# RMSNorm and matmul on one core: casts in groups of eight and four tiles, roots for eight tiles, squares four pairs ahead, no SyncE drains

## The chip, the core and the metric

The kernel runs on one core of a Trainium2 chip. A core has five engines with programs of their own. TensorE multiplies matrices, VectorE (DVE in a profile) and ScalarE (ACT) work on tiles element by element, GpSimd (POOL) is a programmable engine, and SyncE (SP) here only issues transfers. Sixteen DMA engines move data between the chip's memory (HBM) and the core's SBUF. Matmuls write to PSUM, a second small memory. The metric is the device time of one execution in microseconds, the median of several runs. The profile's span is a little shorter than that time, since it runs from the first to the last recorded event.

## The reference

Each of 16 x 1024 rows of 512 numbers is divided by its root mean square, multiplied by gamma, and multiplied by a 512 x 768 matrix:

```python
batch, seq, dim, out_dim = 16, 1024, 512, 768

def reference(x, gamma, weight, eps):
    rms = np.sqrt(np.mean(x ** 2, axis=-1, keepdims=True) + eps)
    x_norm = x / rms * gamma
    return np.matmul(x_norm, weight).astype(np.float32)
```

The input x is 33.6 MB of float32 and the output 50.3 MB.

## The kernel before

The rows are cut into 128 tiles of 128 rows, and the tiles into 64 pairs; a step j of the main loop multiplies pair j, tiles 2j and 2j+1. The division by the root mean square commutes with the matmul, so it is applied when a result leaves PSUM. Gamma is multiplied into the weights once.

A tile goes this way. SyncE loads it as float32, in groups of 16 tiles (`XG`), some groups in one transfer and some in two of eight tiles. GpSimd casts it to bf16. TensorE transposes it, two bf16 at a time seen as one float32 word, and VectorE copies the result from PSUM to SBUF. TensorE multiplies: four blocks of 128 features, each in a part of 512 and one of 256 columns. ScalarE (even tiles) or VectorE (odd tiles) scales the result on its way out of PSUM, and SyncE stores eight tiles at a time. Meanwhile ScalarE squares and sums each tile, takes the root of the means, and VectorE takes the reciprocal.

From the second group on, the last four tiles of each 16 (a "quad") take another way: GpSimd casts them in one instruction and VectorE transposes them in SBUF in 16 moves, three per step.

```python
xin = ctx.enter_context(tc.tile_pool(name="xin", bufs=2))
xbp = ctx.enter_context(tc.tile_pool(name="xb", bufs=4))
stats = ctx.enter_context(tc.tile_pool(name="stats", bufs=4))
tpsum = ctx.enter_context(tc.tile_pool(name="tpsum", bufs=2, space=bass.MemoryType.PSUM))
opsum = ctx.enter_context(tc.tile_pool(name="opsum", bufs=3, space=bass.MemoryType.PSUM))
outp = ctx.enter_context(tc.tile_pool(name="out", bufs=3))
# ... (cut)
def cast(i, engine, n=1):
    if i // 2 not in xb_tiles:
        xb_tiles[i // 2] = xbp.tile([P, 2, D], BF16, name="xb")
    engine.tensor_copy(out=xb_tiles[i // 2][:, i % 2:i % 2 + n, :], in_=held(x_tiles, XG, i, n))

def square(i, ssq):
    jk = junk.tile([P, D], BF16, name="jk")
    nc.scalar.activation(out=jk, in_=held(x_tiles, XG, i)[:, 0, :], func=AF.Square, accum_out=ssq)

def root(i, n, ssq):
    rms = stats.tile([P, 4], F32, name="rms")
    nc.scalar.activation(out=rms[:, :n], in_=ssq[:, :n], func=AF.Sqrt, scale=1.0 / D, bias=eps_sb)
    rstd = stats.tile([P, 4], F32, name="rstd")
    nc.vector.reciprocal(out=rstd[:, :n], in_=rms[:, :n])
    # ... (cut)
# ... (cut)
    load_until(2)
    load_weights(0)
    load_weights(1)
    load_until(2 * XG)
    for _ in range(20):
        nc.sync.drain()
# ... (cut: tiles 0 and 1)
    for j in range(1, NP):
        load_until((2 * j + AHEAD + XG - 1) // XG * XG)
        if j + 3 < NP and quad_of(j + 3) is None:
            cast(2 * j + 6, nc.gpsimd, 2)
        if (2 * j + 2) % XG == 0 and 2 * j + 2 < NT:
            cast_quad((2 * j + 2 + XG - 4) // 4)
        elif 2 * j >= XG:
            move_quad(3)
        if j < 4:
            norms(2 * j + 2, 2)
        if 3 <= j < NP - 2:
            norms_by_four(j + 2)      # squares of pair j+2; a root after every second pair
        if j < 3:
            feed = feeder([j + 1], mid if j == 1 else one, alone=j == 1)
        elif j == 3:
            feed = feeder([4, 5], both)
        elif j + 2 < NP and quad_of(j + 2) is None:
            feed = feeder([j + 2], two)       # transposes of pair j+2 between the matmuls
        else:
            feed = None
        for i, engine in ((2 * j, nc.scalar), (2 * j + 1, nc.vector)):
            a = accumulator()
            matmuls(i, a, range(K), feed)
            finish_tile(i, a, engine)
```

Each engine works through its own program in order. So a ScalarE instruction that waits for data also holds up the evictions behind it, and a TensorE transpose that waits for a cast also holds up the matmuls behind it.

Of the kernel before, what the change touches and what calls it, by code (L numbers as in the profile page):

```python
# [12 lines left out]
F32 = mybir.dt.float32  # L13
BF16 = mybir.dt.bfloat16
# [4 lines left out]
def kernel(  # L19
# [8 lines left out]
    nc = tc.nc  # L28
    P = 128

    x = x.flatten_outer_dims()
    out = out.flatten_outer_dims()
    N, D = x.shape
    _, O = out.shape
    K = D // P
    NT = N // P
    NP = NT // 2
    XG, OG = 16, 8
# [23 lines left out]

    singles = ctx.enter_context(tc.tile_pool(name="singles", bufs=1))
    xin = ctx.enter_context(tc.tile_pool(name="xin", bufs=2))
    xbp = ctx.enter_context(tc.tile_pool(name="xb", bufs=4))
    junk = ctx.enter_context(tc.tile_pool(name="junk", bufs=2))
    stats = ctx.enter_context(tc.tile_pool(name="stats", bufs=4))
    xt_pool = ctx.enter_context(tc.tile_pool(name="xt", bufs=4))
# [6 lines left out]
    x_tiles, xb_tiles, tp_tiles, rstd_of, xT_tiles, o_tiles, norm_sums = {}, {}, {}, {}, {}, {}, {}  # L75

    def held(tiles, group, i, n=1):
        return tiles[i // group][:, i % group:i % group + n, :]
# [8 lines left out]
    def load_until(i):  # L87
        while starts and starts[0] < i:
            load(starts.pop(0))

    def cast(i, engine, n=1):
        if i // 2 not in xb_tiles:
            xb_tiles[i // 2] = xbp.tile([P, 2, D], BF16, name="xb")
        engine.tensor_copy(out=xb_tiles[i // 2][:, i % 2:i % 2 + n, :], in_=held(x_tiles, XG, i, n))  # L94

    def square(i, ssq):
        jk = junk.tile([P, D], BF16, name="jk")
        nc.scalar.activation(out=jk, in_=held(x_tiles, XG, i)[:, 0, :], func=AF.Square, accum_out=ssq)  # L98

    def root(i, n, ssq):  # L100
        rms = stats.tile([P, 4], F32, name="rms")
        nc.scalar.activation(out=rms[:, :n], in_=ssq[:, :n], func=AF.Sqrt, scale=1.0 / D, bias=eps_sb)  # L102
        rstd = stats.tile([P, 4], F32, name="rstd")
        nc.vector.reciprocal(out=rstd[:, :n], in_=rms[:, :n])  # L104
        for t in range(n):
            rstd_of[i + t] = rstd[:, t:t + 1]

    def norms(i, n):
        ssq = stats.tile([P, 4], F32, name="ssq")
        for t in range(n):  # L110
            square(i + t, ssq[:, t:t + 1])
        root(i, n, ssq)


    def norms_by_four(j):
        if j % 2:
            norm_sums[j] = stats.tile([P, 4], F32, name="ssq")
        ssq = norm_sums[j - (j + 1) % 2]
        for t in range(2):
            square(2 * j + t, ssq[:, 2 * (1 - j % 2) + t:2 * (1 - j % 2) + t + 1])  # L120
        if j % 2 == 0:
            root(2 * j - 2, 4, ssq)
        elif j == NP - 1:
            root(2 * j, 2, ssq)

    def transpose_word(j, t, h):
        if j not in tp_tiles:
            tp_tiles[j] = tpsum.tile([P, 2, 2, P], F32, name="tp")  # L130
        words = xb_tiles[j].rearrange("p a d -> p (a d)").bitcast(F32)
        lo = t * (D // 2) + h * P
        nc.tensor.transpose(out=tp_tiles[j][:, t, h, :], in_=words[:, lo:lo + P], identity=ident_f)  # L133

    def evac(j, t=0, n=2):
# [7 lines left out]
    def transpose_tile(i):  # L143
        for h in range(2):
            transpose_word(i // 2, i % 2, h)
        evac(i // 2, i % 2, 1)
# [6 lines left out]
    def quad_of(j):  # L153
        return j // 2 if (2 * j) % XG >= XG - 4 and 2 * j >= XG else None
# [14 lines left out]
    def move_quad(n):  # L169
        for _ in range(min(n, len(quad_moves))):  # L170
            dst, src = quad_moves.pop(0)
            nc.vector.transpose(out=dst, in_=src)  # L172

    def scale(engine, dst, src, r):
        if engine is nc.scalar:
            nc.scalar.mul(out=dst, in_=src, mul=r)  # L176
        else:
            nc.vector.tensor_single_scalar(out=dst, in_=src, scalar=r, op=mybir.AluOpType.mult)  # L178

    def accumulator():  # L180
        return opsum.tile([P, 2, WIDE], F32, name="ops").rearrange("p a b -> p (a b)")
# [16 lines left out]
    def matmuls(i, acc, ks, feed=None):  # L198
        for k in ks:
            matmul(i, k, acc, 0, WIDE)  # L200
            if feed:
                feed()
            matmul(i, k, acc, WIDE, O)

    def finish_tile(i, acc, engine):
        scale(engine, out_tile(i), acc[:, :O], rstd_of[i])
        store(i)
# [16 lines left out]
    with tc.manual_schedule():  # L224
        g_row = singles.tile([2, P, 2], F32)
        nc.scalar.dma_start(out=g_row, in_=gamma.rearrange("(h w c) -> h w c", w=P, c=2))
        nc.scalar.preload_act_table(AF.Sqrt)  # L227
        wv = weight.rearrange("(h w c) o -> w h (c o)", w=P, c=2)
        w_f32 = singles.tile([P, K, O], F32)

        def load_weights(h):
            nc.sync.dma_start(out=w_f32[:, 2 * h:2 * h + 2, :].rearrange("p c o -> p (c o)"), in_=wv[:, h, :])  # L232

        load_until(2)
        load_weights(0)
        load_weights(1)
        load_until(2 * XG)

        for _ in range(20):
            nc.sync.drain()  # L240


        warm = singles.tile([P, WIDE], BF16)
        nc.vector.memset(warm, 0.0)
        eps_sb = singles.tile([P, 1], F32)
        nc.vector.memset(eps_sb, float(eps))  # L246
        ident_f = singles.tile([P, P], F32)
        make_identity(nc, ident_f)
        spare = accumulator()

        def warm_up(n):
            for _ in range(n):
                nc.tensor.matmul(out=spare[:, :WIDE], lhsT=warm[:, :P], rhs=warm, start=True, stop=True)  # L253

        w_bf = singles.tile([P, K, O], BF16)

        def weights(k, engine, lo=0, hi=O):
            scale(engine, w_bf[:, k, lo:hi], w_f32[:, k, lo:hi], g_sb[:, k % 2, k // 2:k // 2 + 1])


        warm_up(6)
        gp = tpsum.tile([P, 2, 2], F32, name="tp")
        for c in range(2):
            nc.tensor.transpose(out=gp[:, c, :], in_=g_row[:, :, c], identity=ident_f[:2, :2])  # L264
        g_sb = singles.tile([P, 2, 2], F32)
        nc.vector.tensor_copy(out=g_sb, in_=gp)  # L266
        cast(0, nc.gpsimd)
        cast(1, nc.gpsimd)
        cast(2, nc.gpsimd, 2)
        norms(0, 2)  # L270
        warm_up(4)
        transpose_tile(0)
        transpose_tile(1)
        warm_up(2)
        weights(0, nc.vector, 0, WIDE)
        weights(0, nc.vector, WIDE, O)
        weights(1, nc.scalar)
        acc = [accumulator() for _ in range(2)]
        for i in range(2):
            matmuls(i, acc[i], [0, 1])  # L280
        weights(2, nc.vector)
        weights(3, nc.scalar)
        norms(2, 2)
        cast(4, nc.gpsimd)
        cast(5, nc.gpsimd)
        matmuls(0, acc[0], [2, 3])
        finish_tile(0, acc[0], nc.scalar)
        matmuls(1, acc[1], [2, 3], feeder([1], [2, 2], alone=True))
        finish_tile(1, acc[1], nc.vector)
        cast(6, nc.gpsimd, 2)  # L290

        mid, one, two, both = ([0, 0, 1, 1, 0, 1, 1, 0], [1, 1, 0, 1, 1, 0, 0, 0], [1, 0, 1, 0, 1, 0, 1, 0],
                               [1, 1, 1, 1, 1, 1, 1, 1])
        for j in range(1, NP):
            load_until((2 * j + AHEAD + XG - 1) // XG * XG)
            if j + 3 < NP and quad_of(j + 3) is None:
                cast(2 * j + 6, nc.gpsimd, 2)
            if (2 * j + 2) % XG == 0 and 2 * j + 2 < NT:
                cast_quad((2 * j + 2 + XG - 4) // 4)
            elif 2 * j >= XG:  # L300
                move_quad(3)
            if j < 4:
                norms(2 * j + 2, 2)
            if 3 <= j < NP - 2:
                norms_by_four(j + 2)
            if j < 3:
                feed = feeder([j + 1], mid if j == 1 else one, alone=j == 1)
            elif j == 3:
                feed = feeder([4, 5], both)
            elif j + 2 < NP and quad_of(j + 2) is None:  # L310
                feed = feeder([j + 2], two)
# [6 lines that stand above are left out]
# [35 lines left out]
```

## Time and profile before

| | before |
|---|---|
| time, median of 3 runs | 210.53 us (210.35 to 210.74) |
| span of the profiled run | 208.4 us |
| granted TensorE clock, mean | 0.985 |
| moved by DMA | 85.68 MB, mean 411 GB/s |
| GpSimd casts of pairs and single tiles | 52, 51.3 us |
| squares on ScalarE | 128, 79.1 us |
| roots on ScalarE, reciprocals on VectorE | 35 and 35, 10.5 and 6.1 us |
| SyncE drains | 20, from 4.6 to 5.7 us |

How to read the lines. In a timeline the columns are the start in us, the length in us, the engine, the line of the kernel, the operation, the output and inputs by their names with shapes, how many instructions are merged, and in brackets how long the engine had been idle and what released it. PE is TensorE and PEld its loading of stationary operands. In the kernel before, L94 is the cast, L98 the square, L102 the root, L104 the reciprocal, L133 the transpose, L140 its copy out of PSUM, L172 the moves of a quad, L176 and L178 the scaling on ScalarE and VectorE, L191 the stores, L194 the matmuls and L83 the loads of x. A group's line gives count, busy time, mean of one in ns, and the idle time before with its releasers. The chain of waits follows back from the last instruction to what released it.

### The profile page before, as it was taken

The page shows a single profiled execution, that of the slowest core. Times are in us where ns is not written, and L with a number is a line of the kernel's source. Part 1 is how long each engine was busy: PE and PEld are TensorE (multiplying, and loading weights), DVE is VectorE, ACT ScalarE, POOL GpSimd, SP SyncE. Part 2 cuts the span into 40 slices and gives each one's busy share as a digit, 9 for nine tenths or more (in the row PEclk, how much of TensorE's full clock was granted, in tenths as well). Part 3 has the DMA queues.
Part 4 walks back from the last instruction along what each step waited for, and adds up shares of the span by engine and source line. Part 5 has one row for each costly group of instructions (what it writes and reads, how often), then busy time and mean ns, then how long its engine had stood idle before and what let it go on. Part 6 is the DMA issues. An engine that isn't in the chain of part 4 may idle for free.

```text
span 208.4 us, 3474 instructions
## 1 busy us (share of the span) xinstructions
PE 193.8 (93%) x1238; PEld 129.3 (62%) x1238; DVE 150.8 (72%) x270; ACT 149.8 (72%) x358; POOL 64.7 (31%) x65
## 2 busy tenths in 40 slices
PE   7699999998999999999999999999999999999800
PEld 3367767764766667666766667666776666766400
DVE  0465657997399957998499957998499957998300
ACT  4698787778678787778778887778778885887300
POOL 3247554002920383055210563016510265000000
PEclk9999999999999999999999999999999999999985
DMA  6999999999999999999999999999999999998992
GB/s 251 421 435 443 343 391 436 463 429 399 417 445 434 410 439 417 418 448 424 432 423 424 437 421 439 418 421 435 440 431 410 442 428 434 437 410 354 419 417 104
DMA packets 5493, 85.68 MB, mean 411 GB/s; under 512 B 610, under 2 KB 612, under 8 KB 1380
## 3 DMA queue, kind: packets, MB, share of 16 engines
q1 hardware_dynamic: 5472, 85.46, 97.0%
q8 instruction: 9, 0.15, 0.3%
q14 instruction: 8, 0.07, 0.1%
q10 hardware_dynamic: 4, 0.00, 0.0%
HBM read 35.13 MB, written 50.33 MB: 410 GB/s over the span
## 4 chain that ended last, share of the span: by engine, by line
PE 78%; DMA 14%; POOL 1%; DVE 1%; SPq 1%; issue 1%; POOLq 0%
PE ops L194 69%; DMA xt<-in_x_dram 14%; PE tp L133 9%; POOL xb L94 1%; DVE ot L178 1%; SPq L232 0%; SPq L83 0%; SPq L191 0%; POOLq L94 0%; DVE xT L140 0%
## 5 line engine op out<-in xcount | busy, mean ns | idle before, releaser
L194 PE MATMUL ops<-w_bf,xT 128*128 128x512 bf16 (+1 forms) x800 | 147.6, 326 | 1.0 <-DVE w_bf L178 0.8
L194 PEld LDWEIGHTS <-xT 128*128 128x128 bf16 x800 | 78.3, 98 | 46.9 <-issue 1.1
L176 ACT ACTIVATE ot<-ops,rstd 128x768 f32<-128x768 f32 x64 | 57.7, 902 | 41.6 <-PE ops L194 39.3
L94 POOL CAST xb<-xt 128x1024 bf16<-128x1024 f32 (+1 forms) x52 | 51.3, 1010 | 98.9 <-DMA xt<-in_x_dram 50.1
L98 ACT ACTIVATE jk<-xt 128x512 bf16<-128x512 f32 x128 | 79.1, 622 | 1.9 <-DMA xt<-in_x_dram 1.7
L178 DVE TENSOR_SCALAR ot<-ops,rstd 128x768 f32<-128x768 f32 x64 | 64.6, 1010 | 9.5 <-PE ops L194 9.1
L133 PE MATMUL tp<-ident_f,xb 128*128 128x128 f32 x200 | 53.9, 273 | 1.4 <-POOL xb L94 1.4
L140 DVE COPY xT<-tp 128x1024 bf16<-128x1024 bf16 (+1 forms) x53 | 34.7, 656 | 25.2 <-PE tp L133 24.5
L172 DVE STREAM_TRANSPOSE xTq<-xq 32x256 f32<-32x256 f32 x112 | 48.7, 435 | 1.9
L194 PE MATMUL ops<-w_bf,xTq 128*128 128x512 bf16 x224 | 42.8, 326 | 0.0
L133 PEld LDWEIGHTS tp<-ident_f,xb 128*128 128x128 f32 x200 | 28.0, 141 | 5.1 <-POOL xb L94 2.6
L194 PEld LDWEIGHTS <-xTq 128*128 128x128 bf16 x224 | 22.0, 98 | 12.4
L98 ACT ACTIVATION_READ_ACCUMULATOR jk<-xt 128x1 f32 x128 | 24.6, 192 | 0.0
L158 POOL CAST xq<-xt 128x2048 bf16<-128x2048 f32 x7 | 13.3, 1896 | 11.4 <-DMA xt<-in_x_dram 9.6
L102 ACT ACTIVATE rms<-ssq,eps_sb 128x4 f32<-128x4 f32 (+1 forms) x35 | 10.5, 299 | 1.1
L104 DVE RECIPROCAL rstd<-rms 128x4 f32<-128x4 f32 (+1 forms) x35 | 6.1, 175 | 6.3 <-ACT rms L102 5.5
L253 PE MATMUL ops<-warm 128*128 128x512 bf16 x12 | 4.4, 505 | 1.2 <-DVE eps_sb L246 1.2
L176 ACT ACTIVATE w_bf<-w_f,g_sb 128x768 bf16<-128x768 f32 x2 | 1.9, 937 | 1.3 <-DMA w_f<-in_weight_dram 1.3
L253 PEld LDWEIGHTS <-warm 128*128 128x128 bf16 x12 | 1.2, 118 | 2.5 <-DVE eps_sb L246 1.2
L266 DVE COPY g_sb<-tp 128x4 f32<-128x4 f32 x1 | 0.2, 164 | 3.2 <-PE tp L264 3.2
L227 ACT ACT_TABLE_LOAD x1 | 1.3, 1283 | 1.3 <-PEq L334 1.3
L178 DVE TENSOR_SCALAR w_bf<-w_f,g_sb 128x512 bf16<-128x512 f32 (+2 forms) x3 | 1.4, 483 | 0.8 <-DMA w_f<-in_weight_dram 0.8
(10 smaller groups left out, 1.9 us busy)
## 6 DMA issues: line engine op xcount, KB each, us to landing
out_dram<-ot SPq DMA_DIRECT2D x13, 3072.0 KB, 18.4
xt<-in_x_dram SPq DMA_DIRECT2D x11, 2048.0 KB, 18.9
xt<-in_x_dram SPq DMA_DIRECT2D x2, 4096.0 KB, 21.4
out_dram<-ot SPq DMA_DIRECT2D x5, 1536.0 KB, 10.9
w_f<-in_weight_dram SPq DMA_DIRECT2D x2, 768.0 KB, 5.5
out_dram<-ot SPq DMA_DIRECT2D x2, 768.0 KB, 17.0
xt<-in_x_dram SPq DMA_DIRECT2D x2, 512.0 KB, 5.1
xt<-in_x_dram SPq DMA_DIRECT2D x1, 1024.0 KB, 9.1
```

What stands on the lines that cost most here:

```text
L94: engine.tensor_copy(out=xb_tiles[i // 2][:, i % 2:i % 2 + n, :], in_=held(x_tiles, XG, i, n))
L98: nc.scalar.activation(out=jk, in_=held(x_tiles, XG, i)[:, 0, :], func=AF.Square, accum_out=ssq)
L102: nc.scalar.activation(out=rms[:, :n], in_=ssq[:, :n], func=AF.Sqrt, scale=1.0 / D, bias=eps_sb)
L104: nc.vector.reciprocal(out=rstd[:, :n], in_=rms[:, :n])
L133: nc.tensor.transpose(out=tp_tiles[j][:, t, h, :], in_=words[:, lo:lo + P], identity=ident_f)
L140: nc.vector.tensor_copy(out=dst[:, t:t + n, :], in_=src[:, t:t + n, :])
L158: nc.gpsimd.tensor_copy(out=quads[q], in_=held(x_tiles, XG, 4 * q, 4))
L172: nc.vector.transpose(out=dst, in_=src)
L176: nc.scalar.mul(out=dst, in_=src, mul=r)
L178: nc.vector.tensor_single_scalar(out=dst, in_=src, scalar=r, op=mybir.AluOpType.mult)
L194: nc.tensor.matmul(out=acc[:, lo:hi], lhsT=xT_tiles[i // 2][:, i % 2, k // 2, :, k % 2], rhs=w_bf[:, k, lo:hi], start=(k == 0), stop=(k == ...
L253: nc.tensor.matmul(out=spare[:, :WIDE], lhsT=warm[:, :P], rhs=warm, start=True, stop=True)
```

## The change

The change makes three engines' programs shorter. GpSimd casts eight tiles with one instruction, and the four that are left of a group before its quad with another; the bf16 buffers become two of eight tiles instead of four of two. ScalarE takes one root for eight tiles (ten at the end) in place of four, and VectorE one reciprocal. For that, the squares run four pairs ahead of the matmuls instead of two, so that the last pair of a group of roots is squared before the first is needed. The 20 drains on SyncE go.

```diff
-    xbp = ctx.enter_context(tc.tile_pool(name="xb", bufs=4))
+    xbp = ctx.enter_context(tc.tile_pool(name="xb", bufs=2))
@@ cast: tiles of the bf16 buffer
-        if i // 2 not in xb_tiles:
-            xb_tiles[i // 2] = xbp.tile([P, 2, D], BF16, name="xb")
-        engine.tensor_copy(out=xb_tiles[i // 2][:, i % 2:i % 2 + n, :], in_=held(x_tiles, XG, i, n))
+        if i // 8 not in xb_tiles:
+            xb_tiles[i // 8] = xbp.tile([P, 8, D], BF16, name="xb")
+        engine.tensor_copy(out=xb_tiles[i // 8][:, i % 8:i % 8 + n, :], in_=held(x_tiles, XG, i, n))
@@ squares and roots (ssq, rms and rstd become [P, 10])
-    def norms_by_four(j):
-        ...
+    NORM_GROUPS = [(5, 2), (7, 4)] + [(f, 4) for f in range(11, NP - 5, 4)] + [(NP - 5, 5)]
+    norm_first = {f + n: (f, s) for f, s in NORM_GROUPS for n in range(s)}
+    norm_turns = {3: [5], 4: [6], 5: [7, 8], 6: [9, 10], **{j: [j + 4] for j in range(7, NP - 6)}, NP - 6: [NP - 2, NP - 1]}
+
+    def norms_of_group(j):
+        first, size = norm_first[j]
+        if j == first:
+            norm_sums[first] = stats.tile([P, 10], F32, name="ssq")
+        ssq = norm_sums[first]
         for t in range(2):
-            square(2 * j + t, ...)
+            square(2 * j + t, ssq[:, 2 * (j - first) + t:2 * (j - first) + t + 1])
+        if j == first + size - 1:
+            root(2 * first, 2 * size, ssq)
@@ after the first loads
-        for _ in range(20):
-            nc.sync.drain()
@@ before the main loop
-        cast(4, nc.gpsimd)
-        cast(5, nc.gpsimd)
+        cast(4, nc.gpsimd, 2)
@@ in the main loop
-            if j + 3 < NP and quad_of(j + 3) is None:
-                cast(2 * j + 6, nc.gpsimd, 2)
+            if j == 1:
+                cast(8, nc.gpsimd, 8)
+            elif j % 8 == 4 and j + 4 < NP:
+                cast(2 * j + 8, nc.gpsimd, 8)
+            elif j % 8 == 6 and j + 2 < NP:
+                cast(2 * j + 12, nc.gpsimd, 4)
...
-            if 3 <= j < NP - 2:
-                norms_by_four(j + 2)
+            for pair in norm_turns.get(j, []):
+                norms_of_group(pair)
```

Cut in this diff: the tile shapes of `root` and `norms`, the body of `norms_by_four`, and the new index of `transpose_word` into the larger bf16 buffer.

More of the change, by code (lines that the diff above doesn't have):

```diff
@@ L100, in root @@
     def root(i, n, ssq):
-        rms = stats.tile([P, 4], F32, name="rms")
+        rms = stats.tile([P, 10], F32, name="rms")
         nc.scalar.activation(out=rms[:, :n], in_=ssq[:, :n], func=AF.Sqrt, scale=1.0 / D, bias=eps_sb)
-        rstd = stats.tile([P, 4], F32, name="rstd")
+        rstd = stats.tile([P, 10], F32, name="rstd")
         nc.vector.reciprocal(out=rstd[:, :n], in_=rms[:, :n])
@@ L108, in norms @@
     def norms(i, n):
-        ssq = stats.tile([P, 4], F32, name="ssq")
+        ssq = stats.tile([P, 10], F32, name="ssq")
         for t in range(n):
@@ L112, in norms @@
         root(i, n, ssq)
-    def norms_by_four(j):
-        if j % 2:
-            norm_sums[j] = stats.tile([P, 4], F32, name="ssq")
-        ssq = norm_sums[j - (j + 1) % 2]
-        for t in range(2):
[L120 to L124, printed above, removed]
+    NORM_GROUPS = [(5, 2), (7, 4)] + [(f, 4) for f in range(11, NP - 5, 4)] + [(NP - 5, 5)]
[6 more added lines that the diff above has]
+        ssq = norm_sums[first]
+        for t in range(2):
+            square(2 * j + t, ssq[:, 2 * (j - first) + t:2 * (j - first) + t + 1])
+        if j == first + size - 1:
+            root(2 * first, 2 * size, ssq)
     def transpose_word(j, t, h):
@@ L130, in transpose_word @@
             tp_tiles[j] = tpsum.tile([P, 2, 2, P], F32, name="tp")
-        words = xb_tiles[j].rearrange("p a d -> p (a d)").bitcast(F32)
-        lo = t * (D // 2) + h * P
+        words = xb_tiles[j // 4].rearrange("p a d -> p (a d)").bitcast(F32)
+        lo = (j % 4 * 2 + t) * (D // 2) + h * P
         nc.tensor.transpose(out=tp_tiles[j][:, t, h, :], in_=words[:, lo:lo + P], identity=ident_f)
```

## The prediction

> **What bounds the kernel now.** I read the page first, then the chain of waits, then the stretches where the chain leaves TensorE. Page, parts 1 and 2:
>
> ```profile
> PE 193.8 (93%) x1238; PEld 129.3 (62%) x1238; DVE 150.8 (72%) x270; ACT 149.8 (72%) x358; POOL 64.7 (31%) x65
> DMA  6999999999999999999999999999999999998992
> GB/s 251 421 435 443 343 391 436 463 429 399 417 445 434 410 439 417 418 448 424 432 423 424 437 421 439 418 421 435 440 431 410 442 428 434 437 410 354 419 417 104
> ```
>
> Two resources are nearly full at once, TensorE and the DMA queue; ScalarE, VectorE and GpSimd, where the change removes instructions, are at 72, 72 and 31%. The chain of waits is TensorE from 10.32 us to 197.46 us with one break:
>
> ```profile
> 27.56 1.02 DVE ot L178
> ...
> 28.63 0.33 SPq L191
> ...
> 29.07 21.39 DMA xt<-in_x_dram
> ...
> 50.60 1.05 POOL xb L94
> ...
> 51.70 0.33 PE tp L133
> ```
>
> The reader is to see a 16-tile load (tiles 32 to 47) issued at 29.07, landing at 50.46, a cast of two of its tiles, and TensorE's transposes of pair 16 starting as that cast ends. TensorE waited 0.7 us there (list of waits). Away from it, a step of two tiles takes 3.04 us with four transposes and 2.60 us without, which is the time of its own matmuls.
>
> The other place is the start, in the timeline of GpSimd (start, us, then what; in brackets the wait before) and of TensorE:
>
> ```profile
> 16.70 4.00 POOL L94 CAST xb<-xt 128x1024 bf16<-128x1024 f32 x4 [2.83 <-DMA xt<-in_x_dram]
> 17.79 0.14 PEld L133 LDWEIGHTS tp<-ident_f,xb 128*128 128x128 f32 x1 [0.16 <-POOL xb L94]
> ```
>
> The load of tiles 8 to 15 lands at about 16.65; the first two-tile cast ends at 17.74, and TensorE takes it 0.05 us later. TensorE and GpSimd are exactly just-in-time here too.
>
> The end, by windows (start:end, length, busy us of each engine, clock, DMA share, GB/s):
>
> ```profile
> 188.00:190.00 2.00, 2.00 (x14) 1.18 (x12) 1.91 (x5) 1.64 (x4) 0.00 (x0) 1.00 0.63 270
> 200.00:202.00 2.00, 0.00 (x0) 0.00 (x0) 0.00 (x0) 0.00 (x0) 0.00 (x0) 1.00 1.08 455
> 188.57 5.10 SPq L191 DMA_DIRECT2D out_dram<-ot  x2
> ```
>
> The queue runs dry at 188 until the store of tiles 112 to 119 is issued at 188.57 (the third line, SyncE's timeline), and is then full until past 204: 3072 + 1536 + 1536 KB, 6.3 MB, at some 430 GB/s are 14.6 us. So the end is fixed by when tile 119 is finished. If TensorE slips, the end slips with it; if TensorE came earlier, the queue would still be busy with the older stores until 188 and nearly nothing would be won.
>
> **What the Trainium skill says.** "Perfetto Trace Analysis", Optimizing Scalar/DVE Operations: grouping into larger operations helps if the engine is saturated, and if it isn't but causes bubbles elsewhere, breaking instructions up lets work finish sooner. GpSimd at 31% is the second case, and this change groups. "DMA: Bandwidth & Descriptors", Queues, rings and completion order: on each DMA engine descriptors are consumed in ring order. The trace agrees: the load of 29.07 took 21.39 us for 4 MB, 10 us at the rate seen, because older work stood before it. "SBUF — State Buffer", SBUF: two separate sides: a GpSimd and a VectorE instruction can block each other for a whole instruction on a shared port. No sign of it here: every two-tile cast takes 1041 to 1045 ns.
>
> **The change part by part.** Groups by form give the price of a cast:
>
> ```profile
> L94 POOL CAST xb<-xt 128x1024 bf16<-128x1024 f32 x48 | 49.0, 1042 | 94.7 <-DMA xt<-in_x_dram 45.9 <-PE tp L133 26.0 <-PE ops L194 22.8
> L158 POOL CAST xq<-xt 128x2048 bf16<-128x2048 f32 x7 | 13.3, 1896 | 11.4 <-DMA xt<-in_x_dram 9.6 <-DVE xTq L172 1.8
> L94 POOL CAST xb<-xt 128x512 bf16<-128x512 f32 x4 | 2.3, 615 | 4.1 <-DMA xt<-in_x_dram 4.1
> ```
>
> From 1024 to 2048 elements 0.854 us more, so 4096 elements take 1.896 + 2 x 0.854 = 3.60 us (estimate). Casts of this line go from 52 to 20 (2 of one tile, 3 of two, 8 of eight, 7 of four): 1.2 + 3.1 + 28.8 + 13.3 = 46.5 us instead of 51.3. GpSimd waits for data anyway, so the 4.8 us are worth nothing; the granularity counts. A consumer of the first pair now waits 3.60 us after the landing instead of 1.04: +2.56 us, wherever the first pair was just in time.
>
> (a) Start, tiles 4 and 5: one cast of 1.04 instead of two of 0.61, the first transpose 0.4 us later; swallowed by (b).
> (b) Start, pair 4: the cast of tiles 8 to 15 ends at 16.70 + 3.60 = 20.30 instead of 17.74. TensorE stands for 2.56 us. Everything after is 2.56 us later (estimate).
> (c) Pair 16. The load's landing does not move although its issue does. By 29.07 SyncE had issued 14.7 MB (32 tiles of x 8.39, weights 1.57, stores of tiles 0 to 11 4.72). Windows up to 29 us give 10.9 MB moved (334, 442, 422, 377, 320 GB/s over 10, 7, 4, 4, 4 us). So 3.8 MB, 9 us of work, stand before the load; issuing it 2.56 us later changes nothing, and it still lands at 50.46. The cast of tiles 32 to 39 then ends at 50.60 + 3.60 = 54.20, transposes at 54.30 instead of 51.70: +2.6 us. TensorE by itself would be there at 51.70 - 0.7 + 2.56 = 53.56, so it waits 0.7 us again. The two delays overlap; they do not add.
> (d) Squares four pairs ahead. ScalarE's timeline before:
>
> ```profile
> 44.09 0.90 ACT L176 ACTIVATE ot<-ops,rstd 128x768 f32<-128x768 f32 x1 [0.91 <-PE ops L194]
> 44.89 0.62 ACT L98 ACTIVATE jk<-xt 128x512 bf16<-128x512 f32 x1
> ...
> 46.91 0.90 ACT L176 ACTIVATE ot<-ops,rstd 128x768 f32<-128x768 f32 x1 [0.36 <-PE ops L194]
> ...
> 50.54 0.63 ACT L98 ACTIVATE jk<-xt 128x512 bf16<-128x512 f32 x1
> ...
> 51.91 0.30 ACT L102 ACTIVATE rms<-ssq,eps_sb 128x4 f32<-128x4 f32 x1
> ```
>
> The evictions are those of tiles 22 and 24 (so step 12 began at 46.91 - 0.05 - 1.30 = 45.5 on TensorE), the squares at 44.89 those of step 12, those at 50.54 the squares of pair 16 in step 14. With the change pair 16 comes in step 12, at 44.89 + 2.56 = 47.5, and ScalarE stands until 50.54, with the eviction of tile 24 behind. Two squares take 1.3 us (50.54 to the root at 51.91, less its gap), the eviction 0.90: done at 52.75. Three accumulators rotate, so tile 27 needs the one of tile 24. TensorE would start tile 27 at 45.5 + 2.56 + 3 x 1.30 = 51.96; it waits 0.8 us, ends tile 27 at 54.1 and meets the transposes of pair 16 at 54.3. That is the same instant as in (c): again an overlap.
> (e) Later groups. Slack grows, because loads are bound by the queue and TensorE is now 2.6 us later. Eight steps take 6 x 3.04 + 2 x 2.60 = 23.44 us; step 14 begins at 51.4, so step 20 at 69.65. Pair 24: data at 71.30 (GpSimd's timeline, like the next), step 20 now at 69.65 + 2.6 = 72.3, so ScalarE does not wait; the cast ends at 74.9 and the transposes come at 77.8. Tightest after that is the last group: data at 165.19, step 52 at 69.65 + 4 x 23.44 + 2.6 = 166.0.
> (f) Roots: 35 to 20, 15 x 0.30 us on ScalarE and 15 x 0.175 us on VectorE. 4.5 and 2.6 us of busy time; each has idle time in most steps. VectorE is full only while it moves quads (5.8 of 6 us in 34 to 46); there two of three reciprocals go, 0.35 us per group, and TensorE was not waiting for it.
> (g) The 20 drains run from 4.6 to 5.7 us, after the last early load is issued at 4.5 and 7 us before the first store at 12.77: nothing.
>
> Sum: 2.6 us on the path. Span 208.4 to 211.0; the time is 2.1 us above the span before, so **213.1 us**, a ratio of 1.012.
>
> **The rivals.** First: the delays add, (b) 2.6 and (c) or (d) 2.6 more less the 0.7, 4.5 us, 215.0 us. This needs the landing of the 16-tile load to move with its issue. Its issue does hang on tile 11 (chain), but 3.8 MB of older work speak against it; I give it 7%. Second: the pool is faster with one long cast, or its landing is earlier than I read, so that the wait is nearer 1.9 us, (b) alone less the 0.7 us gap: 212.4. This happens if the last packets of the load land a little earlier, which the queue allows, since by windows it moved only 354 and 395 GB/s in 46 to 48 and 48 to 50 us. Third: the shorter programs relieve something that bounds (ScalarE, VectorE), and the kernel gains. Against it: TensorE has 0.7 us of waiting after 10.3, and the queue holds old stores until 188, so at most some 0.5 us could come: 210.0. Fourth: deeper squares free the input buffer earlier, so loads are issued earlier (SyncE waited 7.7 us in all for ScalarE before loads, at most 1.6 at once). But data already arrives early and the queue is full: hidden.
>
> **Range and chances.** The 2.6 us rest on one extrapolated duration (within 0.1) and one landing (within about 0.8), the floor is 1.9 us and doubling is unlikely: 212.2 to 214.3 us. Over 2% slower means above 214.74, only by the adding of delays: 0.07. Over 2% faster needs 4.2 us that neither TensorE nor the queue has to give: 0.01. Within 2%: 0.92.
>
> **What would show it.** Right: one GpSimd cast of 128x4096 at 16.7 lasting 3.6 us, TensorE idle some 2.5 us just before 20.3 on a release by that cast; a wait of ScalarE's square for a load ending at about 50.5; TensorE waiting some 0.7 us before 54.3; no other wait of TensorE over 0.5 us; the last store issued 2.6 us later and the same 10 us from there to the end. Step (c) is wrong if the load lands past 52. (b) is wrong if TensorE runs through 17.8 to 20.3. (e) is wrong if TensorE waits again near 75 or 169. The whole is wrong if the store of tiles 112 to 119 is issued later than now and the end does not follow.

## The result and the profile after

| | before | after |
|---|---|---|
| time, median of 6 runs each | 210.45 us | 215.69 us (215.44 to 216.07) |
| ratio | 1 | 1.0248, 95% interval 1.0235 to 1.0261 |
| span of the profiled run | 208.4 us | 213.7 us |
| last store issued | 198.54 us | 206.66 us |

The change makes the kernel 5.2 us slower. The predicted 213.1 us, with a range to 214.3, is too low. Parts 1 and 2 of the page of the changed kernel:

```profile
PE 195.3 (91%) x1214; PEld 130.1 (61%) x1238; DVE 149.4 (70%) x255; ACT 144.8 (68%) x343; POOL 59.8 (28%) x33
DMA  6999999999999999999999999999999999591896
GB/s 252 428 440 439 309 432 428 467 390 436 409 452 336 419 437 423 423 403 437 436 408 423 451 419 437 416 420 426 432 437 417 437 432 414 242 442 74 373 442 294
```

ScalarE, VectorE and GpSimd have less to do, as intended: 5.0, 1.4 and 4.9 us. The DMA queue is short of work between 180 and 187 us and all but empty in slice 37, around 194 us. So TensorE's results came too late for it. The waits of TensorE (engine, what waited, for whom; total, times, longest):

```profile
PE ops L196 <- DVE ot L180: 4.4, 4, 1.1
PE tp L135 <- POOL xb L94: 2.5, 3, 1.8
```

The second line is the wait for long casts that was expected; one of its three, before the transposes of pair 4, is 1.81 us long. The first is new: four times a matmul waits for VectorE's eviction of an accumulator (L180; two lines were added above it). TensorE's timeline shows these four, always the first matmul of a tile (two of them here) and always 1.11 us:

```profile
54.74 0.38 PE L196 MATMUL ops<-w_bf,xTq 128*128 128x512 bf16 x1 [1.11 <-DVE ot L180]
...
126.93 0.38 PE L196 MATMUL ops<-w_bf,xTq 128*128 128x512 bf16 x1 [1.11 <-DVE ot L180]
```

And VectorE's timeline around the first of them:

```profile
51.10 1.02 DVE L180 TENSOR_SCALAR ot<-ops,rstd 128x768 f32<-128x768 f32 x1
...
53.67 1.02 DVE L180 TENSOR_SCALAR ot<-ops,rstd 128x768 f32<-128x768 f32 x1 [1.08 <-PE ops L196]
```

The reader is to see that VectorE was idle for 1.08 us before 53.67, waiting for TensorE. At 53.67 it evicts tile 27, ends at 54.69, and only then does TensorE begin tile 28. Neither engine is full. They take turns on one accumulator, although there are three.

The reason is in the program as built. The kernel asks a pool of three PSUM buffers for an accumulator, and which one it gets is settled when the program is built. The buffers of tiles 22 to 31, counted 0 to 2, as the two built programs list them:

```
tile     22 23 24 25 26 27 28 29 30 31
before    2  0  1  2  0  1  2  0  1  2
after     2  0  1  2  0  2  2  1  0  2
```

Before, the three go strictly in turn, for all 128 tiles. After, tile 27 gets the buffer of tile 25 and tile 28 that of tile 27. The same buffer twice running comes at tiles 28, 76, 92 and 108, which are the four waits. A buffer again after two tiles comes at 27, 43, 45, 59, 61, 75, 91 and 107. How the change in the three engines' programs leads to this order when the program is built is not shown.

How late each tile is evicted, against the kernel before, from the two timelines: tile 8 by 2.63 us (22.83 to 25.46), tile 28 by 3.20 (53.26 to 56.46), tile 62 by 3.64, tile 78 by 5.13, tile 94 by 6.63, tile 127 by 8.12 (197.46 to 205.58). The steps of 1.49 us are groups with the same buffer twice running, those of 0.22 us groups with a buffer again after two.

TensorE is 8.12 us later, and the last store, from SyncE's timelines of the two kernels, as well:

```profile
198.54 0.33 SPq L191 DMA_DIRECT2D out_dram<-ot  x1
206.66 0.33 SPq L193 DMA_DIRECT2D out_dram<-ot  x1
```

But the span is only 5.2 us longer (213.67 less 208.44 us). 2.9 us went back at the end.

### The profile page after: what moved, and what is told of

It reads as the page before. It is cut to its first block, busy times and chain, and to the rows that moved or that the text cites. A ratio compares the mean times of both kernels' runs of the same rounds, so it can differ in the third digit from the quotient of the medians.

```text
span 213.7 us, 3309 instructions
## 1 busy us (share of the span) xinstructions
PE 195.3 (91%) x1214; PEld 130.1 (61%) x1238; DVE 149.4 (70%) x255; ACT 144.8 (68%) x343; POOL 59.8 (28%) x33
## 4 chain that ended last, share of the span: by engine, by line
PE 55%; DVE 29%; DMA 6%; issue 4%; POOL 2%; SPq 1%; DVEq 0%
PE ops L196 48%; DVE ot L180 14%; DVE xTq L174 11%; PE tp L135 7%; DMA xt<-in_x_dram 6%; DVE xT L142 3%; POOL xb L94 2%; SPq L83 1%; DVE rstd L104 1%; SPq L234 0%; DVEq L180 0%
## 5 line engine op out<-in xcount | busy, mean ns | idle before, releaser
L196 PE MATMUL ops<-w_bf,xT 128*128 128x256 bf16 (+1 forms) x783 | 147.5, 325 | 1.7 <-DVE w_bf L180 0.5
L94 POOL CAST xb<-xt 128x4096 bf16<-128x4096 f32 (+3 forms) x20 | 46.2, 2322 | 115.1 <-DMA xt<-in_x_dram 92.7
L180 DVE TENSOR_SCALAR ot<-ops,rstd 128x768 f32<-128x768 f32 x64 | 64.8, 1013 | 11.6 <-PE ops L196 10.9
L196 PE MATMUL ops<-w_bf,xTq 128*128 128x256 bf16 (+1 forms) x217 | 42.4, 324 | 4.8 <-DVE ot L180 4.4
L135 PEld LDWEIGHTS tp<-ident_f,xb 128*128 128x128 f32 x200 | 28.5, 143 | 11.5 <-POOL xb L94 4.9
L104 DVE RECIPROCAL rstd<-rms 128x8 f32<-128x8 f32 (+3 forms) x20 | 3.9, 193 | 7.4 <-ACT rms L102 7.1
L102 ACT ACTIVATE rms<-ssq,eps_sb 128x8 f32<-128x8 f32 (+3 forms) x20 | 6.0, 299 | 0.6
L252 PE MATMUL ops<-warm 128*128 128x512 bf16 x12 | 5.2, 587 | 1.2 <-DVE eps_sb L245 1.2
L180 DVE TENSOR_SCALAR w_bf<-w_f,g_sb 128x512 bf16<-128x512 f32 (+2 forms) x3 | 1.4, 481 | 0.1
```

The source lines that it names most:

```text
L94: engine.tensor_copy(out=xb_tiles[i // 8][:, i % 8:i % 8 + n, :], in_=held(x_tiles, XG, i, n))
L196: nc.tensor.matmul(out=acc[:, lo:hi], lhsT=xT_tiles[i // 2][:, i % 2, k // 2, :, k % 2], rhs=w_bf[:, k, lo:hi], start=(k == 0), stop=(k == ...
```

## The experiments

All were timed against the kernel before on the same chip; its median was 210.4 us each time.

**The changed kernel with the accumulators in turn.**

```diff
-    opsum = ctx.enter_context(tc.tile_pool(name="opsum", bufs=3, space=bass.MemoryType.PSUM))
+    opsum = ctx.enter_context(tc.tile_pool(name="opsum", bufs=1, space=bass.MemoryType.PSUM))
+    turn = iter("012" * 43)
-        return opsum.tile([P, 2, WIDE], F32, name="ops").rearrange("p a b -> p (a b)")
+        return opsum.tile([P, 2, WIDE], F32, name="ops" + next(turn)).rearrange("p a b -> p (a b)")
```

Three named buffers of one instead of a pool of three. Nothing else is changed.

> The changed kernel with its three accumulators taken strictly in turn. Theory A (the program as built takes one accumulator three tiles running at tiles 28, 76, 92 and 108, so TensorE waits for VectorE's eviction): the four waits of 1.11 us go, the last store is issued 2.6 to 3.3 us later than in the kernel before instead of 8.1, time 212.0 to 213.3 us. Theory B (ScalarE's squares standing for a load, and VectorE full while it moves quads, hold the evictions whatever the accumulator): the waits change their name only, time 215.2 to 215.8 us.

Measured: 210.36 us, ratio 0.9997 (0.9987 to 1.0007). The whole 5.2 us are gone. TensorE's waits in this run:

```profile
PE tp L136 <- POOL xb L95: 2.8, 3, 1.8
...
PE ops L197 <- ACT ot L179: 0.4, 1, 0.4
```

Each edit moves the line numbers by one or two: here L197 is the matmul, L136 the transpose, L95 the cast and L179 ScalarE's scaling. The waits for VectorE's evictions have gone, and 0.4 us for one of ScalarE's is all that is new: theory B falls. The last store is issued at 200.66, 2.1 us later than before, and still the time is that of the kernel before. That is less than theory A's 212.0 too, so being 2 us late cost nothing. (The expectation's "three tiles running" is a slip: the same accumulator comes twice running.)

**The kernel before with the changed kernel's order of accumulators.** The same edit on the kernel before, with the 129 buffers written out as the changed program had them.

> The kernel before, with the accumulators in the order that the changed kernel was built with, and nothing else changed. Theory A: TensorE waits about 1.1 us at tiles 76, 92 and 108 and less at 28, the last store 4 to 5 us later, time 212.3 to 214.0 us. Theory B: the accumulators' order alone costs nothing, 210.3 to 210.8 us.

Measured: 214.03 us, ratio 1.0161 (1.0134 to 1.0187). The order alone does it:

```profile
PE ops L195 <- DVE ot L179: 4.4, 4, 1.1
```

The same four waits, in a kernel with none of the change's casts, squares or roots. The last store is issued at 205.0, 6.5 us late. That is more than theory A's 4 to 5 us: tile 28 waits the full 1.1 us too.

**The casts alone.** The diff's casts and bf16 buffers on the kernel before.

> The casts of eight and four tiles alone; squares, roots and drains as before. Theory A: TensorE stands 1.8 us before the transposes of pair 4 and is 2.6 us late from there on, again at pair 16 but overlapping; the last store 2.6 us later, time 212.3 to 213.2 us. Theory B2 (the long casts are the whole cost, again in each group): 215 us or more.

Measured: 210.91 us, ratio 1.0018 (1.0008 to 1.0028). TensorE's timeline shows the predicted stand before the transposes of pair 4:

```profile
20.25 0.33 PE L133 MATMUL tp<-ident_f,xb 128*128 128x128 f32 x1 [1.80 <-POOL xb L94]
```

The eviction of tile 8 is 2.45 us late and the last 1.85. The time grows by 0.5 us only, below what theory A expected. The built program has its accumulators in turn, and its trace has no wait for an eviction, so the casts do not bring the disorder.

**The squares, roots and drains alone.** The changed kernel with the casts of before.

> The squares four pairs ahead, roots of eight and no drains; casts as before. The program as built takes one accumulator twice running at tiles 28, 44, 76, 92 and 108. Theory A: no wait at the start, five waits of about 1.1 us on VectorE's evictions, the last store 5 to 6.5 us later, time 213.0 to 214.8 us. Theory B2 (the long casts are the whole cost): 210.3 to 211.0 us.

Measured: 214.72 us, ratio 1.0196 (1.0172 to 1.0219), as theory A expected; the last store is 6.9 us later, a little more than it said. Five tiles get the buffer of the tile before, and there are five waits:

```profile
PE ops L196 <- DVE ot L180: 5.5, 5, 1.1
```

**TensorE made late on purpose.** In the kernel before, the first matmul of tile 80 is repeated 10 times, or 30. The repeats' results are overwritten by the tile's own first matmul, so nothing is left out.

```diff
                 a = accumulator()
+                for _ in range(10 if i == 80 else 0):
+                    nc.tensor.matmul(out=a[:, :WIDE], lhsT=xT_tiles[i // 2][:, 0, 0, :, 0], rhs=w_bf[:, 0, :WIDE],
+                                     start=True, stop=True)
                 matmuls(i, a, range(K), feed)
```

> The kernel before with 10 matmuls of 512 columns repeated at tile 80, so that TensorE is 2.2 us late from step 40 on. Theory A (the end belongs to the slowest DMA engine's queue, which still holds older stores when the store of tiles 112 to 119 is issued; TensorE may be some 2 to 2.8 us late for nothing): 210.3 to 211.0 us. Theory R (the prediction's: the end follows TensorE): 212.4 to 213.0 us.

> The same with 30 repeated matmuls, TensorE 6.5 us late from step 40 on. Theory A: 6.5 less 2 to 2.8, 214.2 to 215.1 us, as with the accumulators out of turn in the kernel before. Theory R: 216.7 to 217.3 us.

Measured: 210.69 us (ratio 1.0017, 1.0005 to 1.0030) and 215.32 us (1.0226, 1.0204 to 1.0249). The first 2 us of lateness cost 0.3 us; 30 repeats, with the last store 6.7 us late, cost 4.9. The prediction's theory R falls. The slack is real but not one number. With the time of issue of the last store, and its landing as the traces have it (198.5 and 207.5 us in the kernel before), the profiled runs give the table below. The trace counts the landing of each transfer in sixteen parts, as many as there are DMA engines; the last column is the time from the first part of the last store to the sixteenth.

| run | last store issued later by | landed later by | its parts landed over |
|---|---|---|---|
| before | 0 | 0 | 3.0 us |
| 10 repeats | 1.5 us | 0.1 us | 1.6 us |
| casts alone | 1.9 us | 0.5 us | 1.7 us |
| changed, in turn | 2.1 us | -0.3 us | 0.6 us |
| before, out of turn | 6.5 us | 4.4 us | 1.0 us |
| 30 repeats | 6.7 us | 5.7 us | 2.0 us |
| squares and roots alone | 6.9 us | 4.0 us | 0.2 us |
| changed | 8.1 us | 5.2 us | 0.2 us |

So 1.4 to 2.4 us are free in the small cases, and 1.0 to 2.9 us in the large. The last column says where they come from. In all these runs the first part lands 6.0 us after the issue. In the kernel before the slowest part follows 3.0 us later, and what a run gets back is what has gone of these 3.0 us: 2.9 us in the changed kernel, where the sixteen parts land almost together, and 1.0 us with 30 repeats, where one part is again 2.0 us behind the first.

**Smaller last stores.** Tiles 112 to 119 stored as four and four, the last eight as 4, 2 and 2, first in the changed kernel with accumulators in turn, then in the kernel before.

```diff
-    o_first, o_size = stretches(OG, {0: [2, 2, 4], 1: [4, 4], last: [4, 4]})
+    o_first, o_size = stretches(OG, {0: [2, 2, 4], 1: [4, 4], last - 1: [4, 4], last: [4, 2, 2]})
```

> The changed kernel with the accumulators in turn, and the last two store groups cut smaller: tiles 112 to 119 in two stores of four, the last eight as 4, 2 and 2. If the queue is short of work at 188 to 192 us because the store of eight waits for its last tile, the two stores fill it: 0.5 to 1.5 us less than with the accumulators in turn alone, 208.9 to 209.9 us. If the slowest DMA engine has work all the time, no change, 210.1 to 210.6 us.

> The kernel before with the same cut of the last two store groups. Short of work at 188 to 190 us: 0.3 to 1.5 us less, 209.0 to 210.2 us. Otherwise no change, 210.3 to 210.7 us.

Measured: 210.52 us (1.0013, 1.0002 to 1.0024) and 210.49 us (1.0005, 0.9996 to 1.0015). Nothing is won. The stores could start earlier, but the kernel ended no earlier. The parts show it: in the kernel before, the store of tiles 120 to 123 landed from 200.8 to 203.9 us, and with the smaller stores ahead of it from 198.5 to 204.2. The first part came 2.3 us earlier, and the slowest did not.

**Squares and roots in turn.** Squares four pairs ahead, roots of eight, no drains, casts as before, accumulators in turn.

> Squares four pairs ahead, roots of eight, no drains, casts as before, and the accumulators strictly in turn. Theory A: the 4.3 us of the same kernel without the fixed turn go, 210.1 to 210.8 us. Theory B (the deeper squares and the roots of eight themselves hold the evictions): 213 us or more.

Measured: 210.92 us, ratio 1.0030 (1.0011 to 1.0049), against 214.72 without the fixed turn: 3.8 of the 4.3 us are the order. TensorE's timeline shows the prediction's step (d) by itself:

```profile
52.54 1.46 PE L197 MATMUL ops<-w_bf,xT 128*128 128x512 bf16 x8 [2.84 <-ACT ot L179]
```

ScalarE stands for the load of pair 16 with the eviction of tile 24 behind it, and tile 27 waits for it. Here the wait is 2.84 us, because TensorE was not already late from the start; in the changed kernel with accumulators in turn it is 0.43. Its last eviction is 2.3 us late, nearly within the slack.

**Squares ahead, roots of four.** The squares, roots and drains alone once more, but with roots of four tiles; this program was built with its accumulators in turn.

```diff
-    NORM_GROUPS = [(5, 2), (7, 4)] + [(f, 4) for f in range(11, NP - 5, 4)] + [(NP - 5, 5)]
+    NORM_GROUPS = [(f, 2) for f in range(5, NP - 1, 2)] + [(NP - 1, 1)]
```

> Squares four pairs ahead and no drains, casts as before, but roots of four tiles; the program as built has its accumulators in turn by itself. Theory A (it is the order, and the order comes with the roots of eight, not with the distance of the squares): 210.1 to 210.8 us. Theory B (the distance of the squares makes ScalarE stand for the loads): 213 us or more.

Measured: 211.75 us, ratio 1.0057 (1.0036 to 1.0077). A miss: I expected no loss. The trace is of the slowest of five executions (213.22 us, mean clock 0.970; the fastest took 211.11 us at 0.990). Two lines of it, VectorE's and TensorE's timelines:

```profile
52.47 0.18 DVE L104 RECIPROCAL rstd<-rms 128x4 f32<-128x4 f32 x1 [3.93 <-ACT rms L102]
53.28 2.72 PE L196 MATMUL ops<-w_bf,xT 128*128 128x512 bf16 x8 [3.70 <-ACT ot L178]
```

With roots of four, a root follows the squares of pair 16 in step 12, and its reciprocal stands on VectorE too, for 3.93 us. Then neither engine evicts, and TensorE waits 3.70 us. With roots of eight the root comes in step 14. So squares further ahead do cost by standing for a load, as theory B said, only at this one place and less than the order. How much of the 1.4 us is the wait and how much the lower clock after it (last section) is not separated.

**The drains.** The kernel before without them, and with 40.

> The kernel before without the 20 drains, nothing else. All theories: they end 7 us before SyncE's next issue, 210.3 to 210.6 us.

> The kernel before with 40 drains on SyncE in place of 20. If what the drains cost is the fetch of SyncE's longer program by a DMA engine (8 packets of the second instruction queue with 20 drains, 7 without), the time goes with that count: 210.3 to 210.6 us if there are 8 still, 210.7 to 211.0 us if there are 9. If it is the drains' own time, 20 more cost as much as the first 20: 210.8 to 211.0 us. If the 0.2% were chance, 210.3 to 210.6 us with any count.

Measured: 209.94 us without (0.9980, 0.9969 to 0.9992), 210.35 us with 40 (0.9996, 0.9983 to 1.0009). Taking the drains away alone is the only version that beats the kernel before, by 0.2%. It is not the drains' own time, since 20 more cost nothing. Packets of the second instruction queue on the pages of the kernel with 20 drains, and of the one without:

```profile
q14 instruction: 8, 0.07, 0.1%
```

```profile
q14 instruction: 7, 0.06, 0.1%
```

With 40 there are 8, as with 20. In these three the times go with the count, but the changed kernel with accumulators in turn has 5 packets and no drains, and takes 210.36 us. So the cause of the 0.2% stays open.

## Why the prediction was wrong

By its steps:

- (a) and (b), the start: right. The cast of eight tiles took 3.60 us (16.77 to 20.37), TensorE stood until 20.43, and was 2.6 us late from tile 8 on, as predicted. It stood for 1.81 us and not 2.5, but tile 4 was 0.6 us late already. The lines of GpSimd and TensorE:

```profile
16.77 3.60 POOL L94 CAST xb<-xt 128x4096 bf16<-128x4096 f32 x1 [2.87 <-DMA xt<-in_x_dram]
20.43 0.33 PE L135 MATMUL tp<-ident_f,xb 128*128 128x128 f32 x1 [1.81 <-POOL xb L94]
```

- (c), pair 16: right on the data. The load was issued 2.6 us later (31.70) and GpSimd took its data at 50.36, where 50.60 was before. The wait of 0.7 us for its cast, expected again, did not come: with accumulators in turn the cast ends at 53.76 and the transposes begin at 53.81, without a wait.
- (d), the squares: right on ScalarE, wrong on the accumulators. ScalarE took up the squares of pair 16 at 50.30 after standing 2.68 us for the load, and with the accumulators in turn tile 27 waits 0.43 us (0.8 predicted):

```profile
50.30 0.63 ACT L98 ACTIVATE jk<-xt 128x512 bf16<-128x512 f32 x1 [2.68 <-DMA xt<-in_x_dram]
...
52.26 1.46 PE L197 MATMUL ops<-w_bf,xT 128*128 128x512 bf16 x8 [0.43 <-ACT ot L179]
```

  The first line is of the changed kernel, the second of the one with accumulators in turn. But the sentence "Three accumulators rotate" was taken from the kernel's text and from the kernel before. In the changed program they do not rotate. This is **the step that failed**: VectorE's eviction of one tile, 1.02 us, came onto TensorE's path once for each such tile. It made TensorE 5.5 us later (8.12 less 2.63 us) and not the 0 to 0.1 us the sum had beyond the start.
- (e), later groups: nearly right. The data of pair 24 was taken at 72.62, not 71.30, and with accumulators in turn ScalarE waited 0.81 us for it. TensorE waited for no load in any of them.
- (f), the roots: right. ScalarE's went from 10.5 to 6.0 us and VectorE's reciprocals from 6.1 to 3.9, for no gain. What was overlooked is that they change the order of accumulators: with squares ahead and roots of four it stays in turn, with roots of eight it does not.
- (g), the drains: no effect was predicted, a gain of 0.45 us was measured without them, of unknown cause.
- The end: wrong, and in the other direction. "If TensorE slips, the end slips with it" rested on a mean. Windows of the changed kernel with accumulators in turn, the last two columns DMA share and GB/s:

```profile
188.00:190.00 2.00, 1.95 (x14) 1.27 (x13) 1.92 (x4) 0.56 (x1) 0.00 (x0) 1.00 0.52 221
190.00:192.00 2.00, 2.00 (x15) 1.22 (x13) 1.94 (x4) 0.90 (x1) 0.00 (x0) 1.00 0.52 221
```

The kernel before had 0.63 and 270 at 188 to 190, then 0.93 and 393. So on average the DMA engines are idle for a third of 188 to 190 us in the one, where the store of tiles 112 to 119 is issued at 188.57, and for half of the time in the other, where it is issued at 190.69. But the store before it, issued at 176.16, landed in the kernel before in parts from 187.6 to 192.8 us, as its trace tells: some of the 16 engines still had old work, and a transfer has landed when its slowest part has. A mean share of 0.63 was read as an empty queue. The prediction's own sum had the gap in it: 188.57 and 14.6 us are 203.2 us, and the last store landed at 207.5. The changed kernel shows what empty is:

```profile
194.00:196.00 2.00, 1.95 (x14) 1.27 (x13) 1.92 (x4) 0.56 (x1) 0.00 (x0) 1.00 0.00 0
```

There the last store lands 6.1 us after its issue, 9.0 in the kernel before: nothing is left to take up a delay. That lateness of 1.5 to 2.4 us costs at most 0.5 us is shown by five runs: 10 repeats, the casts alone, and the three with the change's squares and roots and accumulators in turn. That it is the slowest engines' old work that hides it is read from the sixteen landings; why some engines lag is not shown, and no run evened them out. The prediction named the sign for this itself: the store of tiles 112 to 119 is issued later and the end does not follow.

The two errors have opposite signs. The start's 2.6 us, for which the prediction stood, costs next to nothing by itself (0.5 us with the casts alone). The order, which it did not contain, costs the 5.2 us. The first rival, at 215.0 us, has about the measured number, but not its mechanism: the delays of the start and of pair 16 overlapped, as predicted.

## What to carry to other kernels

A pool of n buffers is not a promise that they go in turn: after any change in the order of a program, list which buffer each tile gets, and name the buffers one by one where the order matters. Before an engine's delay is put onto the end of a kernel, ask when the slowest part of the transfer before the last one lands, and not only how busy the queue is on average. Work taken from engines with idle time brought nothing here, and the larger instructions and moved waits that came with it could cost.

## What the runs showed of the hardware that was not expected

After a wait of 3.70 us, TensorE's next eight matmuls took 2.72 us, and after one of 2.84 us the same eight took 1.46 us. A window of the former (roots of four); the third column from the end is the granted clock:

```profile
53.00:56.00 3.00, 2.72 (x9) 1.34 (x9) 1.11 (x2) 3.00 (x9) 3.00 (x3) 0.50 1.01 434
```

In that trace the clock fell to 0.50 at 51.7 us, 2.1 us after TensorE's last matmul had ended (49.58), and came back at 58.5, 5.2 us after the matmuls had begun again. In the other, with accumulators in turn and roots of eight, it stayed at 1.00 over the wait of 2.84 us. At the end of that same run it fell 2.1 us after the last matmul, and at the ends of all fourteen profiled runs after 2.1 to 5.3 us. So the length of an idle time does not by itself tell here whether the clock is lost; 2.1 us are the shortest after which it was.
